# A two-layer encoder kernel: two conditioning blocks moved behind the router, expert rows kept in their order

## The chip, the cores and the metric

The kernel runs on one core of a Trainium2 chip. The metric is the device time of one execution in microseconds (us); lower is better. The core has five engines with instruction streams of their own: PE (TensorE, matrix products), DVE (VectorE), ACT (ScalarE), POOL (GpSimd) and SP (SyncE, which here issues the weight transfers). PEld is PE's weight load. DMA engines move data between device memory and the on-chip memory, and the products are accumulated in a small on-chip memory of their own (PSUM).

## What is computed

Two layers over 256 tokens of width 1024. Each layer has a mixer (linear projections, a bidirectional recurrent branch and an attention branch, merged by gates, an output projection) and a mixture of 32 experts of which each token takes two. Both halves are modulated by a conditioning vector `c`: six vectors per layer, shift, scale and gate, come from `w_ada`. Cut to what matters:

```python
cond = silu(c)
mod = cond @ w_ada[l] + b_ada[l]
shift1, scale1, gate1, shift2, scale2, gate2 = split(mod, 6)
h = rms_norm(x, norm1_g[l]) * (1 + scale1) + shift1
proj = h @ w_in[l] + b_in[l]
...                                   # the two branches, merged
x = x + gate1 * (merged @ w_out[l])
h2 = rms_norm(x, norm2_g[l]) * (1 + scale2) + shift2
p_group = softmax(h2 @ w_router_group[l] + b_router_group[l])   # 4 groups, the best one
e_logits = (h2 @ w_router_expert[l] + b_router_expert[l])       # 8 experts in it, the best two
moe = sum over the two experts of weight * (silu(h2 @ w_gate) * (h2 @ w_up)) @ w_down
x = x + gate2 * moe
```

After the second layer a last `rms_norm` is written out. All weights are float32. `mod` is 12 blocks of 512 columns per layer, two to a vector: blocks 0 to 3 are shift1 and scale1, 4 and 5 gate1, 6 and 7 shift2, 8 and 9 scale2, 10 and 11 gate2. A block's weights are 2 MB, two transfers of 1 MB.

## The kernel before, in words

**Weights.** SP issues the weight transfers in the order of a list, `plan`. Each takes a free place of a ring of 1 MB places (`arena`, 16 of which some hold other data for part of the time; three places `y`, which are `B` in the expert stage; two of `X`) and waits where there is none (`pump`, `fits`, `release`, `withhold`). A place comes free when the last product that reads it is done. When the expert stage begins, nearly all places are open to it.

**Order.** The orders of PE and SP are written out by hand: the instructions of these two stand as the program issues them. Those of DVE, ACT and POOL are placed by a list scheduler by priority (`tc.high_priority` raises it).

**Mixer of a layer** (`mixer`). The activations `xs` (2 x 128 tokens) are turned to columns by 16 products with diagonal matrices `dg` that hold the row scale (`pxt`, L664), and `build` makes from them the input of the projections, each value as a high part `hh` and a low part `hl`. The projections are done in steps (`dense`): a step's weights are cast to a high part by ACT (L495), the rest, the low part, is formed by DVE and POOL (L477), and PE does 24 products of 256 columns (L535). Which step and which piece of the branches follow on each other on PE is a string per layer, `MIX`: a number is so many dense steps, a name is a piece of a branch, and `r6` or `c2` is an ada block of this layer (row) or of the next (column).

**An ada block.** `row(b)` calls `ada_part`: eight products (`pada`, L410) give four partial sums on 128 partitions, ACT copies the sum to a high part (L414), DVE takes the rest (L415). After the next dense step `ada_sum` adds the partitions up by two products with ones (`prow`, L442), and DVE adds the row to `g1b`, `sh2b`, `A2b` or `gt2b` (gate1, shift2, scale2, gate2, each broadcast over the partitions). In layer 1, which has all 12, `MIX` places r4 to r11 in the mixer, and c0 to c3 for the next layer; layer 2 has r6 to r11 there.

**Merge and output projection.** After the last word of `MIX` come eight dense steps of the merge (`pm`, L523) and eight of the output projection (`pd`, L550), in four column pieces n of two steps. Between merge steps 4 and 5 PE turns the row `sh2b` to columns twice, in two orders, by one-row products (`psh` and `psj`, L1064 and L1069); the first serves the router's constant `lc`, the second the rows of the experts. `fin_wo` adds a piece to `xs` and makes `xa` (the row times scale2), `xa_T` turns it (`pxa`), `logits` does the router's products (`pL`, L1089).

**Router and experts** (`experts`). DVE does the row scale for both token halves at once (`rstd_of`), then softmax, the choice of group and experts, and the places of the tokens (`onehot`, L1218), with PE's counting products `pp` (L1180) between. ACT makes the scaled rows `xp[0]` (L1139) from `xa`, reading it in strides to bring it into the order in which the expert weights lie, and DVE the low part `xp[1]` (L1392), both of them in token halves. Then 16 pairs of experts follow, each with `wg`, `wu`, `wd` of 2 MB an expert: gather (`pG`, L1240, once for two pairs), gate and up (`pgu`, L1268), down (`pd`, L1293), scatter (`psc`, L1313). The gather is released by `onehot` and `xp`; the row gate2, `gt2b`, is needed first by the scatter of the first pair.

## Time and profile before

| | us |
|---|---|
| median of 3 runs | 1503.98 |
| lowest and highest | 1502.64, 1508.92 |
| profiled execution, its time | 1508.72 |
| its span in the profile | 1507.0 |
| granted clock of PE over the span | 0.965 |
| PE busy | 1358.7 (90%) |
| DVE busy | 642.6 (43%) |
| ACT busy | 396.0 (26%) |
| POOL busy | 275.9 (18%) |
| weight transfers (SP's queue) | 517.00 MB, 86.4% of the DMA engines' time |

The profile is one execution, and its rows add up to its own span; the time lies 1.7 us above the span. The profiled execution is 4.7 us longer than the median of the three. A share of the whole span says little here, since the program alternates between two kinds of stage: the mixers lie at about 34 to 294 us and 778 to 1020 us, the expert stages behind them. Windows of one stage show which engine is full in it. A row of the trace has the start in us, the duration, the engine, the line, the operation, output <- input and shapes, how many instructions stand in the row (x24), and in brackets how long the engine stood idle ahead of it and what ended that. Neighbours of one kind are drawn together in one row, and a product in full float32 (`pada`, `psh`, `pxt`, `pgu`) counts as two in a trace and as one in the program's order.

### The profile page before, as it was taken

What the parts mean: (1) busy time and instruction counts of PE and PEld (TensorE: products, weight loads), DVE (VectorE), ACT (ScalarE), POOL (GpSimd) and SP (SyncE); (2) the same over time, 40 slices, a digit from 0 to 9 for tenths busy, and PEclk for the clock granted to TensorE, in tenths of its full rate; (3) what the DMA queues carried; (4) which work ended last, traced back from release to release, by engine and by line L of the source; (5) the groups of instructions that cost most, each with busy time, mean ns of one, the idle gap of its engine ahead of it and who ended that gap; (6) DMA issues with size and microseconds to landing.
All of it is one profiled execution on the core that took longest, in us unless ns stands there. A gap on an engine that the chain in (4) does not pass through costs nothing. (4 is left out here: it accounts for less than half of the span.)

```text
span 1507.0 us, 20322 instructions
## 1 busy us (share of the span) xinstructions
PE 1358.7 (90%) x7902; PEld 797.8 (53%) x7903; DVE 642.6 (43%) x1396; ACT 396.0 (26%) x729; POOL 275.9 (18%) x318
## 2 busy tenths in 40 slices
PE   5899999879999989889978999997999999887996
PEld 2877779834434434334347887994434443334432
DVE  1887664632323312223258867554223323213223
ACT  2536554411111101011035366633111111101101
POOL 4644324500000000000015543550000000000000
PEclk9899999989999999989989999998999999999998
DMA  9877687769999999999995657666999999999995
GB/s 330 314 268 245 245 281 281 275 275 422 420 422 421 420 421 422 420 418 375 416 388 193 227 199 256 224 252 227 422 420 421 422 420 422 421 421 419 378 422 218
DMA packets 122633, 522.26 MB, mean 347 GB/s; under 512 B 14068, under 2 KB 16320, under 8 KB 74400
## 3 DMA queue, kind: packets, MB, share of 16 engines
q1 hardware_dynamic: 116448, 517.00, 86.4%
q0 software_dynamic: 1200, 1.99, 0.7%
q10 hardware_dynamic: 4880, 1.87, 0.5%
q8 instruction: 66, 1.08, 0.3%
q14 instruction: 39, 0.32, 0.1%
HBM read 519.77 MB, written 1.05 MB: 346 GB/s over the span
## 5 line engine op out<-in xcount | busy, mean ns | idle before, releaser
L1268 PE MATMUL pgu<-arena 128*64 128x512 f32 x1456 | 349.3, 595 | 20.5 <-DMA arena<-in_w_up_dram 12.0
L1268 PEld LDWEIGHTS pgu<-arena 128*64 128x64 f32 x1456 | 115.4, 137 | 222.8 <-issue 172.8
L1277 DVE SCALAR_TENSOR_TENSOR arena<-pgu,wsl,arena 128x512 f32<-128x512 f32 x32 | 36.4, 1137 | 383.0 <-PE pgu L1268 383.0
L1293 PE MATMUL pd<-arena 128*64 128x512 f32 x720 | 179.8, 597 | 7.3 <-ACT arena L1284 7.3
L1224 POOL TENSOR_TENSOR arena<-oh,arena 128x256 f32<-128x256 f32 x32 | 19.5, 615 | 740.9 <-DVE oh L1218 468.8
L477 POOL TENSOR_TENSOR R<-arena,R 128x512 fp32r<-128x512 f32 (+1 forms) x84 | 124.9, 1490 | 156.3 <-ACT R L495 104.4
L535 PE MATMUL pd<-R,R 128*128 128x256 f32 x1008 | 134.2, 291 | 9.0 <-DVE R L477 5.7
L550 PE MATMUL pd<-R,R 128*128 128x256 f32 x1056 | 136.4, 288 | 2.2 <-DVE R L477 1.9
L535 PEld LDWEIGHTS pd<-R,R 128*128 128x128 f32 x1008 | 127.1, 197 | 18.4 <-issue 6.9
L550 PEld LDWEIGHTS pd<-R,R 128*128 128x128 f32 x1056 | 130.6, 194 | 8.1 <-issue 4.4
L1304 DVE TENSOR_TENSOR y<-pd,arena 128x512 f32<-128x512 f32 x64 | 44.1, 691 | 204.0 <-PE pd L1293 167.7
L1268 PE MATMUL pgu<-B,arena 128*64 128x512 f32 x432 | 118.0, 594 | 2.7 <-DMA B<-in_w_up_dram 2.7
L477 DVE TENSOR_TENSOR R<-arena,R 128x512 fp32r<-128x512 f32 (+1 forms) x100 | 83.3, 840 | 58.5 <-ACT R L495 53.8
L1293 PEld LDWEIGHTS pd<-arena 128*64 128x64 f32 x720 | 56.0, 138 | 95.3 <-issue 85.5
L1305 ACT CAST yh<-y 128x512 fp32r<-128x512 f32 x64 | 39.6, 619 | 241.9 <-DVE y L1304 241.9
L495 ACT CAST R<-arena 128x1024 fp32r<-128x1024 f32 x76 | 79.4, 1046 | 80.5 <-PE pd L550 26.7
L1316 DVE TENSOR_TENSOR xs<-xs,psc 128x512 f32<-128x512 f32 x128 | 79.3, 680 | 17.9 <-PE psc L1313 17.9
L1240 PE MATMUL pG<-oh,X 128*128 128x256 f32 x512 | 74.3, 309 | 13.2 <-DVE oh L1218 9.0
L1240 PEld LDWEIGHTS pG<-oh,X 128*128 128x128 f32 x512 | 70.8, 215 | 24.2 <-issue 24.2
L1268 PEld LDWEIGHTS pgu<-B,arena 128*64 128x64 f32 x432 | 38.4, 137 | 73.2 <-issue 61.2
L1284 ACT COPY arena<-pat 128x512 f32<-128x512 f32 x32 | 18.7, 585 | 220.1 <-PE pat L1283 220.1
L1244 ACT ACTIVATE arena<-pG,sh2c 128x256 f32<-128x256 f32 x64 | 30.3, 474 | 159.0 <-DVE arena L1246 159.0
(328 smaller groups left out, 1694.4 us busy)
## 6 DMA issues: line engine op xcount, KB each, us to landing
arena<-in_w_up_dram SPq DMA_DIRECT2D x104, 1024.0 KB, 19.8
arena<-in_w_down_dram SPq DMA_DIRECT2D x90, 1024.0 KB, 19.8
arena<-in_w_gate_dram SPq DMA_DIRECT2D x78, 1024.0 KB, 19.8
arena<-in_w_ada_dram SPq DMA_DIRECT2D x36, 1024.0 KB, 6.4
B<-in_w_gate_dram SPq DMA_DIRECT2D x30, 1024.0 KB, 19.8
arena<-in_w_in_dram SPq DMA_DIRECT2D x27, 1024.0 KB, 8.2
B<-in_w_up_dram SPq DMA_DIRECT2D x24, 1024.0 KB, 19.8
X<-in_w_gate_dram SPq DMA_DIRECT2D x20, 1024.0 KB, 19.8
```

The lines of the kernel that those rows point to most:

```text
L477: eng.tensor_tensor(dst, full, hi.bitcast(F32), op=ALU.subtract)
L495: A.copy(wh, w)
L535: T.matmul(acc[key][o][:, 0:S], lhsT=w[:, kk, P * o:P * o + P], rhs=x_[:, 4 * kh + kk], start=kh == 0 and i == 0 and kk == 0, stop=kh == 1 ...
L550: T.matmul(acc[key][t][:, 0:256], lhsT=x_[:, 4 * kh + kk, P * t:P * t + P], rhs=w[:, kk], start=kh == 0 and i == 0 and kk == 0, stop=kh == ...
L1240: T.matmul(pG[:, kk, 0:n], lhsT=x_[:, t, k, :], rhs=oh[:, t, :], start=i == 0, stop=i == 3)
L1244: A.activation(xg[k][:, 0:n], pG[:, kk, 0:n], AF.Identity, bias=sh2c[:, k:k + 1])
L1268: T.matmul(pg[CAP * e:CAP * e + CAP, :], lhsT=xg[4 * h + kk][:, P * (i % 2) + CAP * e:P * (i % 2) + CAP * e + CAP], rhs=w[e][:, kk, :], st ...
L1277: V.scalar_tensor_tensor(ac.rearrange("p k q -> p q k"), pu.rearrange("p (q k) -> p q k", k=4), wsl[:, 0:1], sl.rearrange("p (q k) -> p q ...
L1293: T.matmul(pd[n][CAP * e:CAP * e + CAP, :], lhsT=aT[:, 2 * h + kk, CAP * e:CAP * e + CAP], rhs=w[e][:, kk, 512 * n:512 * n + 512], start=h ...
L1304: V.tensor_tensor(y[:, cs], pd, gt2b[:, cs], op=ALU.mult)
L1305: A.copy(yh[:, cs], y[:, cs])
L1316: V.tensor_tensor(xx, xx, pq, op=ALU.add)
```

## The change

1. **gate2 (blocks 10 and 11)** leaves `MIX` in both layers. Its transfers stand in the plan behind the output projection's weights and ahead of the experts'. Its partial sums follow on PE right behind the last logits and stay in two PSUM tiles; ACT copies them to on-chip memory after the router's chain; their sums over the partitions, one product of ones a block in full float32, stand in the first pair, between its gate and its up products.
2. **shift2 (blocks 6 and 7)** stays in `MIX`, but its partial sums go by one strided ACT copy to the order of the experts (`ada_shift`), and after the next dense step eight small products a block turn and sum them at once (`pshift`, `shift_put`). `psh`, `psj` and the row `sh2b` are gone; the constant `lc` is made from a second copy of the router weights, loaded by POOL's queue in the same order (`wr2`).
3. **Rows of the experts**: a third form of `xa`, `xaP`, lies in the experts' order (slot 6 of the arena, which so comes free with slots 4 and 5 behind the low parts). `fin_wo` makes it, by ACT for n = 0 to 2 and by POOL for n = 3. `xp` is then made without strides.
4. **Router chain first**: row scale, logits and `xp` by token half, the chain under a high priority; the low part of the first half ahead of the chain, that of the second behind `onehot`; `weights()` last. The last piece of the output projection is done token half by token half (`by_rows`).
5. **Rows turned unscaled**: `turn_rows` uses plain transposes of `xs`, in layer 1 ahead of the row scale, for layer 2 around the last scatter of layer 1; the scale is spread over the partitions by two products and applied in `build`.
6. **Other**: casts, low parts and ada copies of the mixer get a higher priority (`PREP`); the ring has one more place during the mixer (`spare`, kind `z`, not for expert weights); some parameters of layer 1 go from POOL's queue to SP's; the `MIX` strings have a dense step moved in a few places.

The diff, cut to its core:

```diff
+GATES = (10, 11)
 FIRST = (0, 2, 1, 3)
+PREP = 60
 ORDER = (("q", 2), ("k", 2), ("akv", 1), ("aq", 2), ("v", 2), ("o", 2), ("gm", 4), ("ga", 4))
...
+        if kind == "z":
+            return key[0] not in ("wg", "wu", "wd", "fin")
+        late = key[0] in ("wg", "wu", "wd", "wm", "wa", "wo") or (key[0] == "ada" and key[2] in GATES)
...
+        for b in GATES:
+            plan_ada(l, b)
...
+        return pb
+
+    def ada_part(l, b):
+        pb = ada_sums(l, b)
         ph, pw = parts_at[0][:, 0, :], parts_at[0][:, 1, :]
-        A.copy(ph, pb)
-        V.tensor_tensor(pw, pb, ph.bitcast(F32), op=ALU.subtract)
+        with tc.high_priority(offset=PREP):
+            A.copy(ph, pb)
+            V.tensor_tensor(pw, pb, ph.bitcast(F32), op=ALU.subtract)
         return ph, pw
...
+    def ada_shift(l, b):
+
+        A.copy(turned_sums, ada_sums(l, b).rearrange("p (q k) -> p k q", k=KD))
+
+    def shift_put(sh2c, b3, b):
+        o = 64 * (b % 2)
+        pc = ps.tile([P, 512], F32, tag="f", name="pshift")
+        for k in range(KD):
+            T.matmul(pc[o:o + 64, 2 * k:2 * k + 2], lhsT=turned_sums[:, k, :], rhs=ones[:, 0:2], start=True, stop=True,
+                     tile_position=(0, o))
+        V.tensor_tensor(sh2c[o:o + 64, :], pc[o:o + 64, 0:2 * KD].rearrange("p (k o) -> p k o", o=2)[:, :, 0],
+                        b3[o:o + 64, :], op=ALU.add)
...
+    def turn_rows(pairs):
+        for kp in pairs:
+            pt = turned_rows[kp] = ps.tile([P, 2, S], F32, tag="c", name="pxt")
+            for kk in range(2):
+                for t in range(NT):
+                    k = 2 * kp + kk
+                    T.transpose(pt[:, kk, t * P:t * P + P], xs[:, t, k * P:k * P + P], ident)
...
-            A.copy(wh, w)
-            low(wl[:, 0:2], w[:, 0:2], wh[:, 0:2], V)
-            low(wl[:, 2:4], w[:, 2:4], wh[:, 2:4], G)
+            with tc.high_priority(offset=PREP):
+                A.copy(wh, w)
+                low(wl[:, 0:2], w[:, 0:2], wh[:, 0:2], V)
+                low(wl[:, 2:4], w[:, 2:4], wh[:, 2:4], G)
...
+                    turns_ = [(i, t) for t in range(NT) for i in range(3)]
+                for i, t in turns_:
...
-                    k = 2 * kp + kk
-                    T.matmul(pt[:, kk, t * P:t * P + P], lhsT=xs[:, t, k * P:k * P + P], rhs=dg[t], start=True,
-                             stop=True)
...
+        def spread():
+            pr = ps.tile([P, 512], F32, tag="f", name="pr")
+            for t in range(NT):
+                T.matmul(pr[:, t * P:t * P + P], lhsT=rx[:, t:t + 1].to_broadcast([P, P]), rhs=ident, start=True,
+                         stop=True)
+            V.tensor_copy(scale, pr[:, 0:S])
...
-                src = pts[k // 2][:, k % 2, :]
-                A.activation(hh[:, k, :], src, AF.Identity, bias=c1[:, k:k + 1], scale=A1[:, k:k + 1])
+                src = turned_rows[k // 2][:, k % 2, :]
                 tmp = rot("htmp", 13, 0, 4, S)
-                V.tensor_scalar(tmp, src, A1[:, k:k + 1], c1[:, k:k + 1], op0=ALU.mult, op1=ALU.add)
-                low(hl[:, k, :], tmp, hh[:, k, :], G if k % 2 else V)
+                V.scalar_tensor_tensor(tmp, src, A1[:, k:k + 1], scale, op0=ALU.mult, op1=ALU.mult)
+                A.activation(hh[:, k, :], tmp, AF.Identity, bias=c1[:, k:k + 1])
+                if k % 2:
+                    A.activation(tmp, tmp, AF.Identity, bias=c1[:, k:k + 1])
+                    low(hl[:, k, :], tmp, hh[:, k, :], G)
+                else:
+                    V.scalar_tensor_tensor(hl[:, k, :], tmp, c1[:, k:k + 1], hh[:, k, :].bitcast(F32), op0=ALU.add,
+                                           op1=ALU.subtract)
...
+            cols = p["cols"]
+            V.tensor_tensor(c1, mods[l], cols[:, 80:96], op=ALU.add)
+            with tc.high_priority(offset=100):
+                spread()
+                build(range(8))
...
+            if b // 2 == 3:
+                ada_shift(l, b)
+                last_sum.append(lambda: shift_put(sh2c, p["b3"], b))
+                return
...
+        sh2c = sm.tile([P, KD], F32, tag="sh2c", name="sh2c")
+        nc.gpsimd.dma_start(wr2[:, :, 0:4], w_rg[l].rearrange("(p k) g -> p k g", k=KD))
+        nc.gpsimd.dma_start(wr2[:, :, 4:36], w_re[l].rearrange("(p k) g -> p k g", k=KD))
...
+        xa, xaP = at(5, 0, NT, D), at(6, 0, NT, KD, P)
...
+            dst = xaP[:, t, :, 32 * n:32 * n + 32].rearrange("p k q -> p q k")
+            if n == 3:
+                G.tensor_tensor(dst, xs[:, t, cs].rearrange("p (q k) -> p q k", k=KD),
+                                A2b[:, cs].rearrange("p (q k) -> p q k", k=KD), op=ALU.mult)
+            else:
+                A.copy(dst, xa[:, t, cs].rearrange("p (q k) -> p q k", k=KD))
...
         dense(4)
-        ph = ps.tile([P, 512], F32, tag="c", name="psh")
-        for k in range(KD):
-            T.matmul(ph[:, 2 * k:2 * k + 2], lhsT=sh2b[0:1, P * k:P * k + P], rhs=ones[0:1, 0:2], start=True, stop=True)
...
-        for k in range(KD):
-            T.matmul(pj[:, 2 * k:2 * k + 2], lhsT=sh2b[0:1, :].rearrange("o (q k) -> o k q", k=KD)[:, k, :],
-                     rhs=ones[0:1, 0:2], start=True, stop=True)
...
         assert not any(r[0] is retired[0] for r in ready)
         region("y", f"B{l}", [F32] * 3, "right")
-        release([("y", s) for s in range(3)] + [("a", 6)])
+        release([("y", s) for s in range(3)])
...
-            T.matmul(pL[0][:, 72:108], lhsT=shT[:, k, 0:1].to_broadcast([P, P]), rhs=wr[:, k, :], start=k == 0,
+            T.matmul(pL[0][:, 72:108], lhsT=sh2c[:, k:k + 1].to_broadcast([P, P]), rhs=wr2[:, k, :], start=k == 0,
...
+        gates_ = [ada_sums(l, b) for b in GATES]
...
         ss2 = small("ss2", NT)
-        V.tensor_reduce(ss2, ssn, axis=AX, op=ALU.add)
-        r = rstd_of(ss2, NT, 1.0 / D)
         L = small("L", NT, 36)
         for t in range(NT):
-            V.scalar_tensor_tensor(L[:, t, :], pL[t][:, 0:36], r[:, t:t + 1], lc, op0=ALU.mult, op1=ALU.add)
-        for t in range(NT):
-            A.activation(xp[0][:, t].rearrange("p k q -> p q k"), xa[:, t, :].rearrange("p (q k) -> p q k", k=KD),
-                         AF.Copy, scale=r[:, t:t + 1])
+            V.tensor_reduce(ss2[:, t:t + 1], ssn[:, t, :], axis=AX, op=ALU.add)
+            r = rstd_of(ss2[:, t:t + 1], 1, 1.0 / D, small)
+            V.scalar_tensor_tensor(L[:, t, :], pL[t][:, 0:36], r, lc, op0=ALU.mult, op1=ALU.add)
+            A.activation(xp[0][:, t], xaP[:, t], AF.Copy, scale=r)
+            if t == 0:
+                V.scalar_tensor_tensor(xp[1][:, t], xaP[:, t], r, xp[0][:, t].bitcast(F32), op0=ALU.mult,
+                                       op1=ALU.subtract)
...
+            if not last:
+                turn_rows(range(2))
             scatter(owT, (1,), close)
+            if not last:
+                turn_rows(range(2, 4))
...
-            V.scalar_tensor_tensor(xp[1][:, t].rearrange("p k q -> p q k"),
-                                   xa[:, t, :].rearrange("p (q k) -> p q k", k=KD), r[:, t:t + 1],
-                                   xp[0][:, t].rearrange("p k q -> p q k").bitcast(F32), op0=ALU.mult,
-                                   op1=ALU.subtract)
-        release([("a", 4), ("a", 5)])
+        with tc.issue_after(marks["oh"].ins):
+            marks["lo"] = V.scalar_tensor_tensor(xp[1][:, 1], xaP[:, 1], r, xp[0][:, 1].bitcast(F32), op0=ALU.mult,
+                                                 op1=ALU.subtract)
+        release([("a", 4), ("a", 5), ("a", 6)])
         gather(oh)
-        weights()
+        urgent.close()
+        sums = [at(9, 512 * i, 512) for i in range(2)]
+        for s, pb in zip(sums, gates_):
+            A.copy(s, pb)
+        with tc.issue_after(marks["lo"].ins):
+            weights()
...
+            if i == 0:
+                for h, s in enumerate(sums):
+                    pc = ps.tile([P, 512], F32, tag="f", name="prow")
+                    T.matmul(pc, lhsT=ones, rhs=s, start=True, stop=True)
+                    g = gt2b[:, 512 * h:512 * h + 512]
+                    V.tensor_tensor(g, g, pc, op=ALU.add)
```

**PE in the mixer of layer 1 and in its merge.** Before, the two turns of the shift stand between two merge steps:

```order
L523 MATMUL pm<-Y_1825,R_158 128x256 x2
L523 MATMUL pm<-Y_1826,R_158 128x256
L523 MATMUL pm<-Y_1825,R_158 128x256
L1064 MATMUL psh<-onesr,arena 128x2 x8
L1069 MATMUL psj<-onesr,arena 128x2 x8
L523 MATMUL pm<-Y_1825,R_157 128x256
L523 MATMUL pm<-Y_1826,R_157 128x256
L523 MATMUL pm<-Y_1825,R_157 128x256 x2
```

After, they are gone from there, and behind the dense step that follows on a shift block's `pada` stands `pshift`:

```order
L428 MATMUL pada<-arena,condp 32x512 x8
L596 MATMUL pd<-R_146,R_144 128x256 x8
L596 MATMUL pd<-R_146,R_145 128x256 x8
L596 MATMUL pd<-R_146,R_144 128x256 x8
L455 MATMUL pshift<-onesr,arena 64x2 x8
L878 MATMUL pqt<-ident,arena 128x128 x4
L596 MATMUL pd<-R_147,R_144 128x256 x8
L596 MATMUL pd<-R_147,R_145 128x256 x8
```

The one-row products left the merge, and two groups of eight products of two columns now stand among the dense steps.

**PE behind the last logits.** `pL` are the router's products, `pxa` the last turned rows, `pp` the counting products, which wait for the router's choice. Before:

```order
L1089 MATMUL pL<-arena 128x36 x4
L1052 MATMUL pxa<-ident,arena 128x128 x4
L1089 MATMUL pL<-arena 128x36 x4
L1180 LDWEIGHTS trisb
L1180 MATMUL pp<-arena,trisb 128x64
L1181 LDWEIGHTS onesb
L1181 MATMUL pp<-arena,onesb 128x32
L1183 LDWEIGHTS onesb
L1183 MATMUL pp<-arena,onesb 128x32
```

After:

```order
L1141 MATMUL pL<-arena 128x36 x4
L1115 MATMUL pxa<-ident,arena 128x128 x4
L1141 MATMUL pL<-arena 128x36 x4
L428 MATMUL pada<-arena,condp 32x512 x16
L1238 LDWEIGHTS trisb
L1238 MATMUL pp<-arena,trisb 128x64
L1239 LDWEIGHTS onesb
L1239 MATMUL pp<-arena,onesb 128x32
L1241 LDWEIGHTS onesb
L1241 MATMUL pp<-arena,onesb 128x32
```

The 16 products of the two gate2 blocks now stand where PE waits for the router's choice.

**DVE in the router's chain of layer 1**, from the logits on (`X` are the expert rows, `ry` the row scale). Before, both low parts (L1392) stand in the chain:

```order
L1158 TENSOR_TENSOR arena<-arena,desc 128x64
L1158 TENSOR_TENSOR arena<-arena,desc 128x8
L1392 SCALAR_TENSOR_TENSOR X_2938<-arena,ry,X_2937 128x128x8
L1160 TENSOR_REDUCE arena<-arena 128x8
L1160 TENSOR_REDUCE arena<-arena 128x2
L1392 SCALAR_TENSOR_TENSOR X_2938<-arena,ry,X_2937 128x128x8
L1162 TENSOR_TENSOR arena<-desc,arena 128x64
L1162 TENSOR_TENSOR arena<-desc,arena 128x8
L1200 TENSOR_REDUCE arena<-arena 128x2
L1170 SCALAR_TENSOR_TENSOR arena<-arena 128x64
```

After, the reductions and comparisons stand token half by token half, and one low part (L1197):

```order
L1194 SCALAR_TENSOR_TENSOR arena<-pL,arena,lc 128x36
L1213 TENSOR_REDUCE arena<-arena 128x8
L1197 SCALAR_TENSOR_TENSOR X_2932<-arena,X_2931 128x1024
L1215 TENSOR_TENSOR arena<-arena 128x64
L1213 TENSOR_REDUCE arena<-arena 128x2
L1216 TENSOR_TENSOR arena<-arena,desc 128x64
L1215 TENSOR_TENSOR arena<-arena 128x8
L1218 TENSOR_REDUCE arena<-arena 128x8
L1216 TENSOR_TENSOR arena<-arena,desc 128x8
L1220 TENSOR_TENSOR arena<-desc,arena 128x64
L1218 TENSOR_REDUCE arena<-arena 128x2
L1228 SCALAR_TENSOR_TENSOR arena<-arena 128x64
```

The low part of the second half left this stretch for the place behind `onehot`, and each remaining step has a half of the tokens' width.

## Rows read from the trace of the kernel before

**Rows 1.** Stage windows: layer 1's experts, layer 2's mixer, its router chain, a piece of layer 1.

```profile
318.30:660.00 341.70, 317.60 (x1525) 135.43 (x1523) 98.23 (x167) 40.40 (x72) 7.95 (x13) 0.99 1.01 419
...
786.00:1022.00 236.00, 224.03 (x1766) 203.00 (x1765) 161.35 (x368) 122.74 (x231) 117.13 (x110) 0.97 0.64 229
...
1022.00:1046.30 24.30, 13.25 (x72) 9.57 (x73) 14.87 (x63) 10.32 (x16) 1.19 (x2) 0.72 0.46 173
...
80.00:100.00 20.00, 18.62 (x144) 16.11 (x144) 18.91 (x62) 7.20 (x9) 8.78 (x11) 1.00 0.74 258
```

**Rows 2.** TensorE in the merge of layer 1 (start, duration, what), and the clock window behind it.

```profile
242.75 3.03 PE L523 MATMUL pm<-Y,R 128*128 128x256 f32 x24
...
245.71 1.94 PE L1064 MATMUL psh<-onesr,arena 1*128 1x2 f32 x16
...
247.52 3.94 PE L1069 MATMUL psj<-onesr,arena 1*128 1x2 f32 x16
...
251.38 5.04 PE L523 MATMUL pm<-Y,R 128*128 128x256 f32 x24
...
250.00:252.00 2.00, 2.00 (x10) 1.99 (x10) 0.51 (x2) 0.00 (x0) 0.17 (x1) 0.50 0.00 0
```

**Rows 3.** TensorE, ada blocks 10 and 11 and their row sums.

```profile
178.14 1.06 PE L410 MATMUL pada<-arena,condp 128*32 128x512 f32 x8 [1.38 <-DMA arena<-in_w_ada_dram]
...
849.60 0.78 PE L442 MATMUL prow<-part,onesr 128*128 128x512 f32 x1 [2.25 <-DVE part L415]
...
902.01 1.92 PE L410 MATMUL pada<-arena,condp 128*32 128x512 f32 x16
...
913.03 0.63 PE L442 MATMUL prow<-part,onesr 128*128 128x512 f32 x2
```

**Rows 4.** Around the sum of block 6 in layer 1: VectorE, then TensorE.

```profile
190.67 3.22 DVE L906 SCALAR_TENSOR_TENSOR arena<-arena,ry 128x128 f32<-128x128 f32 x8
...
194.41 0.67 DVE L477 TENSOR_TENSOR R<-arena,R 128x512 fp32r<-128x512 f32 x1
...
194.55 0.79 PE L442 MATMUL prow<-part,onesr 128*128 128x512 f32 x1 [2.88 <-DVE part L415]
...
199.19 2.85 PE L410 MATMUL pada<-arena,condp 128*32 128x512 f32 x16
```

**Rows 5.** The start of the program, TensorE.

```profile
24.01 5.27 PE L664 MATMUL pxt<-arena,xs 128*128 128x128 f32 x32
...
38.95 1.43 PE L535 MATMUL pd<-R,R 128*128 128x256 f32 x5 [2.44 <-ACT R L495]
```

**Rows 6.** TensorE at the border of the two layers.

```profile
770.66 0.40 PE L1313 MATMUL psc<-yl,owT 128*128 128x512 f32 x1
...
777.78 5.47 PE L664 MATMUL pxt<-arena,xs 128*128 128x128 f32 x32 [3.24 <-DVE arena L650]
...
785.49 3.14 PE L535 MATMUL pd<-R,R 128*128 128x256 f32 x24
```

**Rows 7.** Layer 1 from the last output product on: TensorE, SyncE's queue, a DMA window.

```profile
291.24 3.11 PE L550 MATMUL pd<-R,R 128*128 128x256 f32 x24
...
314.77 7.09 PE L1268 MATMUL pgu<-arena 128*64 128x512 f32 x32
...
296.29 22.97 SPq L168 DMA_DIRECT2D arena<-in_w_up_dram  x4
...
318.00:320.00 2.00, 2.00 (x12) 0.60 (x10) 0.00 (x0) 0.00 (x0) 0.00 (x0) 1.00 0.32 66
```

**Rows 8.** Router chain of layer 1: ScalarE, VectorE, TensorE.

```profile
298.30 3.83 ACT L1139 ACTIVATE X<-arena,ry 128x1024 fp32r<-128x1024 f32 x2 [1.12 <-DVE ry L394]
...
300.36 1.97 DVE L1392 SCALAR_TENSOR_TENSOR X<-arena,ry,X 128x1024 fp32r<-128x1024 f32 x1 [0.76 <-ACT X L1139]
...
306.66 0.23 PE L1180 MATMUL pp<-arena,trisb 128*128 128x64 bf16 x1 [8.56 <-DVE arena L1177]
...
308.45 6.39 PE L1240 MATMUL pG<-oh,X 128*128 128x256 f32 x32 [1.47 <-DVE ci L1213]
```

More of the change, by code (lines that the diff above doesn't have):

```diff
@@ L261, in trunk @@
                 plan_ada(l, EARLY[1])
+            if l == 0 and it == ("q", 0, 1):
+                add(("more", l), lambda: first["p"]["more"](), None)
             if it == ("k", 0, 0):
@@ L376, in setup, with rstd_of @@
         return first["p"]
-    def rstd_of(ss, n, scale):
+    def rstd_of(ss, n, scale, place_=None):
         def t(nm):
-            return sm.tile([P, n], F32, tag=f"{nm}{n}", name=nm)
+            return place_(nm, n) if place_ else sm.tile([P, n], F32, tag=f"{nm}{n}", name=nm)
         v, w, y, u = t("rv"), t("rw"), t("ry"), t("ru")
@@ L412, in ada_part @@
             done("ada", l, b, h)
+        return pb
+    def ada_part(l, b):
+        pb = ada_sums(l, b)
         ph, pw = parts_at[0][:, 0, :], parts_at[0][:, 1, :]
-        A.copy(ph, pb)
-        V.tensor_tensor(pw, pb, ph.bitcast(F32), op=ALU.subtract)
+        with tc.high_priority(offset=PREP):
+            A.copy(ph, pb)
+            V.tensor_tensor(pw, pb, ph.bitcast(F32), op=ALU.subtract)
         return ph, pw
     def ada_fast(b):
-        pb = ps.tile([P, 512], F32, tag="f", name="pada")
-        for h in range(2):
-            w = wt("ada", 0, b, h)
-            for kk in range(4):
-                T.matmul(pb[32 * kk:32 * kk + 32, :], lhsT=condp[:, 4 * h + kk, :], rhs=w[:, kk, :],
-                         start=h == 0, stop=h == 1, tile_position=(0, 32 * kk))
-            done("ada", 0, b, h)
         t = rot("fast", 5, 0, 2, 512)
-        A.copy(t, pb)
+        A.copy(t, ada_sums(0, b))
         return t
+    def ada_shift(l, b):
[8 more added lines that the diff above has]
+                        b3[o:o + 64, :], op=ALU.add)
     def ada_put(c1, cols, b, t):
@@ L546, in fn @@
                     acc[key] = [ps.tile([P, 512], F32, tag="f", name="pd") for _ in range(2)]
-                for i, (w, x_) in enumerate(((wh, sh), (wh, sl), (wl, sh))):
-                    for t in range(NT):
-                        for kk in range(4):
-                            T.matmul(acc[key][t][:, 0:256], lhsT=x_[:, 4 * kh + kk, P * t:P * t + P], rhs=w[:, kk],
-                                     start=kh == 0 and i == 0 and kk == 0, stop=kh == 1 and i == 2 and kk == 3)
-                        if kh == 1 and i == 2:
-                            fin(t, acc[key][t][:, 0:256])
+                parts = tuple(enumerate(((wh, sh), (wh, sl), (wl, sh))))
+                turns_ = [(i, t) for i in range(3) for t in range(NT)]
+                if by_rows and kh == 1:
+                    turns_ = [(i, t) for t in range(NT) for i in range(3)]
+                for i, t in turns_:
+                    w, x_ = parts[i][1]
+                    for kk in range(4):
+                        T.matmul(acc[key][t][:, 0:256], lhsT=x_[:, 4 * kh + kk, P * t:P * t + P], rhs=w[:, kk],
+                                 start=kh == 0 and i == 0 and kk == 0, stop=kh == 1 and i == 2 and kk == 3)
+                    if kh == 1 and i == 2:
+                        fin(t, acc[key][t][:, 0:256])
             queue(key, fn)
@@ L694, in mixer @@
         else:
+            cols = p["cols"]
+            V.tensor_tensor(c1, mods[l], cols[:, 80:96], op=ALU.add)
+            with tc.high_priority(offset=100):
+                spread()
+                build(range(8))
             ada_row(l, EARLY[0], pa)
             pa = ada_part(l, EARLY[1])
-            cols = p["cols"]
-            V.tensor_tensor(c1, mods[l], cols[:, 80:96], op=ALU.add)
-            build(range(8))
         if l:
@@ L1100, in mixer, with experts @@
         logits(3)
+        gates_ = [ada_sums(l, b) for b in GATES]
         dump(f"xm{l}", xs)
+        assert not any(r[1][0] == "z" for r in ring.values())
+        free.remove(("z", 0))
         es.close()
         region("x", f"X{l}", [F32] * 2 + [F32R] * 2)
-        return pL, lc, ssn, xa, sh2c
-    def experts(l, p, pL, lc, ssn, xa, sh2c):
+        return pL, lc, ssn, xaP, sh2c, gates_
+    def experts(l, p, pL, lc, ssn, xaP, sh2c, gates_):
         last = l == depth - 1
```

99 lines of the change are left out of this document (48 added, 51 removed).

## Prediction

> **What bounds the kernel now.** I read the stage windows first [rows 1]. In layer 1's expert products the DMA share is 1.01 at 419 GB/s: 341.7 us in which the transfers never stop. PE is busy for 317.6 of them, but its pauses are waits for weights. A place of 1 MB (1.049 million bytes) takes 1.049 / 0.419 = 2.50 us there. An edit that only makes PE, DVE or ACT shorter in that stage is worth nothing, and one that lets the stream start earlier, or keeps it from stopping, is worth what it adds. In layer 2's mixer the picture is turned round: PE 224.0 of 236.0 us, DMA share 0.64, DVE 161.4, ACT 122.7, POOL 117.1. There PE is the bound, its order is written by hand, and each of its waits (12.0 us in that window) is on the path. Between the two lies the router's chain: PE 13.3 of 24.3 us, DVE 14.9, DMA share 0.46. So I price PE time in the mixers at its full length and PE time in the expert stages at nothing, and then ask what the stream makes of an earlier mixer end.
>
> **a. Starts of the layers: -5.0.** In layer 1 the turns (5.27 us) begin at 24.01, and the first dense step waits 2.44 us for a cast until 38.95 [rows 5]. Unscaled turns move into a time in which PE waits, but the chain behind goes through scale, `build` and casts, so not all 5.27 are won; `build` has also four ACT steps more. Between +2 (the steps, where nothing hides them) and -5.3 I take -2.0. At the border the last scatter ends at 771.06, the turns wait 3.24 us for DVE's row scale and begin at 777.78, and dense starts at 785.49 [rows 6]. The turns now stand around the scatter; what is left between is the scale, its spread by two products, and `build`. Of 7.7 us from 777.78 to dense some 3 should go: -3.0, between -1 and -4.5.
>
> **b. The shift's turns in the merge: -10.2.** `psh` takes 1.94 us, `psj` 3.94, and the merge step behind them 5.04 in place of 3.03 [rows 2]. In the window from 250 the granted clock is 0.50, the 1.2 GHz level: PE spent the time before on products of one row and two columns, with which the rows show it as busy all along. Removed per layer: 245.71 to 251.38 is 5.7, and 2.0 for the slow step, 7.7. Added per layer: two groups of `pshift`, each 16 rows of two columns like `psh`, 1.94 each, and no `prow` for the two blocks, 2 x 0.63 [rows 3]. 7.7 - 3.9 + 1.3 = 5.1 a layer.
>
> The Trainium skill (TensorE: Matmul & The Clock Gate, Part 1: The HAM clock gate) says that the low clock is the default and that activity releases it. With that, small products dropped between dense steps could lower the clock anew, at four places instead of two; the last rival prices this from rows.
>
> **c. The gate blocks leave the mixers: -13.8.** A block costs 1.92 us of `pada` and 0.63 of `prow`, four blocks 10.2 [rows 3]. With them go two waits, 1.38 us for a transfer (layer 1) and 2.25 for DVE's part (layer 2). Behind the logits the same products cost nothing: in layer 1 PE stands idle there for 8.56 us until 306.66 [rows 8], and two blocks need 3.84. If that cover went, they would cost 3.8 a layer. Their row sums stand between gate and up products of the first pair, in the stage that the stream bounds: nothing.
>
> **d. Block 6's sum: -3.8.** In layer 1 `prow` waits 2.88 us for DVE, which does 3.22 us of the branches and a low part first [rows 4]; a block a little later takes 2.85 us, against 1.92, so 0.93 is the slow clock behind the wait. A shift block now needs one ACT copy only. If ACT is as late as DVE was, nothing is won; if the neighbouring step is covered too, 5.4.
>
> **e. What DVE gives back: +2.2.** In the piece at 80 to 100 us DVE is busy 18.91 of 20 us, PE 18.62 [rows 1]. There PE runs no faster than DVE. Two of the blocks of c stand in such pieces, and I take back nearly half of their 5.1 us. The other end, where all of the mixers were so, is a rival.
>
> Together 5.0 + 10.2 + 13.8 + 3.8 - 2.2 = 30.6 us less until the two expert stages begin.
>
> **f. What the stream gives back: +7.0.** The stages end when the last weights are in, so what counts is how many weights have landed at T, the end of the last output product: 291.24 + 3.11 = 294.35 in layer 1 [rows 7]. Before, all 18 places are full well ahead of the first free one: a group of four issues that began at 296.29 ends at 319.26, T + 25, and in the window from 318 the DMA share is 0.32. So the stream stands still until the gate products, which begin at 314.77, return places. After, the gate blocks (4 MB) come first and hold four of the 13 places that are open by T. They return them when their sums are done, some 6 us after T; nine expert places are left to fill, 9 x 2.50 = 22.5 us, and the count that stood at T + 25 is reached at T + 28.5. That is 3.5 us a layer. Between 0 (the places return early, or the stream gets ahead in the mixer, which the DMA share of 0.64 would allow) and 10.0 (all four MB of a layer are added to the full stream) I take 3.5, by the count of places.
>
> **g. The router's chain: 0.** The two low parts cost 1.97 us each on DVE, the two strided scalings 3.83 on ACT, and the gather 6.39 at the low clock [rows 8]. Half widths, no strides and one low part behind `onehot` shorten this by perhaps 4 us a layer, and PE, which now has products to do in the wait, may gather at the high clock. But by f the stream is busy until T + 28.5, and the first places come back at about T + 24 even without any gain: the chain has slack. If f were nothing, the 4 us of each layer would count, and the two sizes bound each other.
>
> The added copies (`xaP`), the loads of the router's second weights and the parameters moved to SP's queue lie in mixers with DMA share 0.64 and ACT 122.7 of 236 us [rows 1]: nothing, or a place's 2.50 us where SP's queue is held up once. The higher priority of casts and low parts (`PREP`) can win from the waits that are left or lose in the branches; both are rivals.
>
> **Sum.** 30.6 - 7.0 = 23.6. The profiled execution took 1508.7, so 1485.1 of its kind; it lies 4.7 above the median of 1503.98, so 1480.4, and I say **1481**. The bounds of a, d and f together, which hardly fall on one side at once, give 1476 to 1487 around it.
>
> **Rivals.**
>
> *The mixers are bound by DVE, not by PE (1491).* Then taking products off PE leaves waits for low parts in their place. For it: 18.91 of 20 in the window at 80. Against it: 161.4 of 236 over layer 2's mixer [rows 1]. It would leave a, b and half of c, 5.0 + 10.2 + 6.9 = 22, less 7 for the stream and 2 for shares of b that fall into such pieces: 13 us. Chance 0.20.
>
> *More waits go (1471).* `PREP` puts casts ahead of branch work, and a dense step rarely waits any more. The window of layer 2 has 12.0 us of idle PE; if layer 1 has as much, 24 in all, of which c and d count 6.5. Half of the remaining 17 is 9 to 10 more. Chance 0.13.
>
> *The clock falls at the new small products (1497).* If each of the four `pshift` groups took 3.94 us like `psj` and slowed the next step by 2.0 [rows 2], that would be 4 x 4.0 = 16 us. Against it: `psh` itself took 1.94, and a single group is short. Chance 0.07.
>
> *The gate blocks' transfers are not absorbed (1500).* If all 8 MB are added to the full stream, 8 x 2.50 = 20 us of the 23.6 come back. It needs the stream to be no further at T than before, less the 4 MB, in spite of a shorter wait. Chance 0.06.
>
> *Slower (1514).* `PREP` puts casts and low parts ahead of the branches' chains on ACT and DVE. A low part on DVE is 0.67 us [rows 4] and a cast about 1.0 (half of a strided scaling of 128x1024 [rows 8]), so a chain step that meets one of each is 1.7 late, and with PE's fixed order the dense steps behind it wait. Of the 30.6 - 7.0 = 23.6 us nothing is left at 14 such meetings in both layers, seven a layer; at ten a layer it is 34 - 23.6 = 10 us slower. Against it: casts always stood in the same queues, and the branches' pieces are spread over dense steps. Chance 0.06, with 0.01 for others.
>
> **Chances.** The forecast has 0.48. A measurement of this kernel can tell about 0.5%, 7.5 us, from no change. Faster by more than that: the forecast, the DVE case, the case of more waits, and a little of the clock's, 0.82. Within it: most of the clock's case, the transfers, and tails, 0.11. Slower: 0.07. The range from 1469 to 1497 holds the first four cases.
>
> **What would show it.** Right: no `psh` and `psj`, the merge steps all at about 3.0 us, clock 1.0 in the merge; `pada` right behind the last logits while DVE is at the router; a DMA share near 1.0 from T + 6 on without the dip at 318; dense 2 to 4 us earlier behind the border; mixers shorter by about 15 us each. Wrong: longer idle rows ahead of dense products with DVE or ACT as the releaser; the dip of the DMA share still there, in which case g counts and f does not; `pshift` rows of 4 us; branch products that wait longer than before.

## The result

The median fell from 1504.64 us (4 runs, 1502.64 to 1508.92) to 1484.13 us (4 runs, 1483.02 to 1484.68). The medians differ by 20.5 us. The ratio of the runs is 0.9859, with a 95% interval of 0.9837 to 0.9881, which is 17.9 to 24.5 us less. The forecast was 1481 with a range from 1469 to 1497. The profiled executions differ by more, 1508.72 to 1483.02 (spans 1507.0 and 1481.1, 25.9 us), since the one of before lies 4.1 us above its median and the one of after 1.1 below.

The table sets both profiled executions side by side at five marks on PE: the first dense product, the end of the last output product (T), the first gate product of the experts, the end of the layer's last scatter, and the end of the program. The last column is what the kernel after is ahead by at that mark.

| mark, us | before | after | gained so far |
|---|---|---|---|
| first dense product | 38.95 | 38.20 | 0.8 |
| T in layer 1 | 294.35 | 278.83 | 15.5 |
| first gate product of layer 1 | 314.77 | 295.68 | 19.1 |
| last scatter of layer 1 ends | 771.06 | 757.85 | 13.2 |
| first dense product of layer 2 | 785.49 | 766.26 | 19.2 |
| T in layer 2 | 1021.36 | 994.06 | 27.3 |
| first gate product of layer 2 | 1041.80 | 1009.42 | 32.4 |
| end | 1507.0 | 1481.1 | 25.9 |

The last column is the finding of this case: it rises in the mixers and at the border, rises again in the router's chain, and falls in both expert stages. From T to the last scatter layer 1 takes 479.0 us in place of 476.7, from T to the end layer 2 takes 487.0 in place of 485.6.

### The profile page after: what moved, and what is told of

The parts are those of the page before. It is cut to its first block, busy times and chain, and to the rows that moved or that the text cites. A ratio compares the mean times of both kernels' runs of the same rounds, so it can differ in the third digit from the quotient of the medians.

```text
span 1481.1 us, 20274 instructions
## 1 busy us (share of the span) xinstructions
PE 1345.1 (91%) x7870; PEld 782.3 (53%) x7871; DVE 630.1 (43%) x1390; ACT 399.4 (27%) x749; POOL 281.2 (19%) x321
## 5 line engine op out<-in xcount | busy, mean ns | idle before, releaser
L1328 PE MATMUL pgu<-arena 128*64 128x512 f32 x1520 | 418.6, 594 | 17.7 <-DMA arena<-in_w_up_dram 14.0
L1328 PEld LDWEIGHTS pgu<-arena 128*64 128x64 f32 x1520 | 138.1, 137 | 235.7 <-issue 179.4
L518 POOL TENSOR_TENSOR R<-arena,R 128x512 fp32r<-128x512 f32 (+1 forms) x73 | 108.4, 1486 | 104.0 <-ACT R L537 80.3
L1328 PE MATMUL pgu<-X,arena 128*64 128x512 f32 x240 | 106.6, 594 | 6.4 <-DMA X<-in_w_up_dram 6.4
L518 DVE TENSOR_TENSOR R<-arena,R 128x512 fp32r<-128x512 f32 (+1 forms) x81 | 75.8, 945 | 59.1 <-ACT R L537 49.7
L1328 PE MATMUL pgu<-B,arena 128*64 128x512 f32 x288 | 87.1, 595 | 7.2 <-DMA B<-in_w_gate_dram 5.9
L1300 PE MATMUL pG<-oh,X 128*128 128x256 f32 x512 | 70.6, 298 | 13.0 <-DVE oh L1278 12.0
L537 ACT CAST R<-arena 128x1024 fp32r<-128x1024 f32 x65 | 67.8, 1045 | 51.5 <-PE pd L596 15.5
L1300 PEld LDWEIGHTS pG<-oh,X 128*128 128x128 f32 x512 | 67.0, 204 | 24.1 <-issue 22.6
L1353 PE MATMUL pd<-B,arena 128*64 128x512 f32 x240 | 70.8, 595 | 3.6 <-ACT arena L1344 3.6
```

The lines of the kernel that those rows point to most:

```text
L518: eng.tensor_tensor(dst, full, hi.bitcast(F32), op=ALU.subtract)
L537: A.copy(wh, w)
L1300: T.matmul(pG[:, kk, 0:n], lhsT=x_[:, t, k, :], rhs=oh[:, t, :], start=i == 0, stop=i == 3)
L1328: T.matmul(pg[CAP * e:CAP * e + CAP, :], lhsT=xg[4 * h + kk][:, P * (i % 2) + CAP * e:P * (i % 2) + CAP * e + CAP], rhs=w[e][:, kk, :], st ...
L1353: T.matmul(pd[n][CAP * e:CAP * e + CAP, :], lhsT=aT[:, 2 * h + kk, CAP * e:CAP * e + CAP], rhs=w[e][:, kk, 512 * n:512 * n + 512], start=h ...
```

## The profile after

Windows of the kernel after. Columns as in rows 1: window, length, busy time and instructions of PE, PEld, DVE, ACT, POOL, granted clock, DMA share, GB/s.

```profile
228.00:248.00 20.00, 20.00 (x170) 20.00 (x169) 14.11 (x17) 8.24 (x13) 12.69 (x12) 1.00 0.73 268
278.00:282.00 4.00, 3.14 (x27) 2.82 (x26) 3.85 (x22) 1.66 (x6) 1.95 (x2) 1.00 0.04 16
282.00:286.00 4.00, 3.74 (x34) 0.99 (x33) 3.79 (x20) 2.85 (x4) 0.00 (x0) 1.00 0.44 119
286.00:290.00 4.00, 0.85 (x7) 0.59 (x7) 3.36 (x11) 1.68 (x2) 0.00 (x0) 1.00 1.02 426
298.00:302.00 4.00, 4.00 (x22) 1.31 (x20) 0.46 (x1) 0.00 (x0) 0.00 (x0) 1.00 1.02 426
299.00:640.00 341.00, 312.68 (x1477) 130.51 (x1474) 96.18 (x162) 39.77 (x69) 7.34 (x12) 0.99 1.01 421
766.26:994.06 227.80, 214.00 (x1727) 195.83 (x1723) 161.25 (x364) 126.67 (x243) 116.77 (x113) 0.99 0.65 230
```

The expert stage is as full of transfers as in rows 1 (1.01, 421 GB/s), and the mixer of layer 2 still is PE's: 214.0 of 227.8 us. In the merge (228 to 248) the clock stays at 1.00, where rows 2 show 0.50. What moved is the hole in the stream, the stretch in which no weights come in. Before, it lies from 310 to 318, ahead of the first places that the experts return; a window of it, of the kernel before:

```profile
312.00:314.00 2.00, 2.00 (x12) 2.00 (x12) 0.55 (x2) 0.47 (x1) 0.00 (x0) 0.56 0.00 0
```

Now it lies around T (0.04 and 0.44 from 278 to 286), and from 286 on the stream does not stop. In layer 2 it lies in the same place: from 994 to 1000 the DMA share is 0.03 or less, from 1002 on 0.85 or more.

TensorE of the kernel after in layer 1, from the merge to the first gate products, and one `pshift`:

```profile
123.80 1.09 PE L455 MATMUL pshift<-onesr,arena 128*64 128x2 f32 x16
...
240.27 3.04 PE L565 MATMUL pm<-Y,Y 128*128 128x256 f32 x24
...
275.72 3.11 PE L596 MATMUL pd<-R,R 128*128 128x256 f32 x24
...
282.10 3.64 PE L428 MATMUL pada<-arena,condp 128*32 128x512 f32 x32
287.78 0.20 PE L1238 MATMUL pp<-arena,trisb 128*128 128x64 bf16 x1 [2.04 <-DVE arena L1235]
...
290.52 5.23 PE L1300 MATMUL pG<-oh,X 128*128 128x256 f32 x29 [0.51 <-DVE X L1456]
295.68 3.65 PE L1328 MATMUL pgu<-arena 128*64 128x512 f32 x16
```

T is 275.72 + 3.11 = 278.83. The gate blocks' 3.64 us fit into the wait for the router's choice, of which 2.04 us are left, against 8.56 in rows 8. In layer 2 they take 5.3 us, from 997.33 to 1002.67, in a stretch with the clock at 0.50 in part, and 0.34 us of the wait are left: there they only just fit. The chain from T to the first gate product shrank from 20.4 to 16.9 us, in layer 2 to 15.4.

## The experiments

Four questions stood open. Is the stream what gives time back, and does it hide the router's chain? What is the shift's part worth alone? Where does the border's gain come from, which is twice the forecast? Did the raised priority do anything? Each ratio is taken against runs of the kernel before made beside it; their medians are 1505.49 (the first four), 1505.86 (the part alone, the turned rows, the priority) and 1504.24 (the late turns).

**Gate blocks back in the mixers.** The strings `MIX` are those of before, the blocks' plan position and their sums behind the logits are gone:

```diff
-        for b in GATES:
-            plan_ada(l, b)
...
-        gates_ = [ada_sums(l, b) for b in GATES]
+        gates_ = []
```

> The changed kernel with one part undone: blocks 10 and 11 are summed in the mixers again, where they stood before, and nothing of them stands behind the logits. Theory (the stream and the router's chain share one slack): the two output projections end about 11 to 12 us later in sum, but no gate block holds a place, so the 3.7 us that the stream gave back return, and the chain, shorter by 3.6 and 5.1 us than before, now sets when places come free and counts: 11.6 - 3.7 - 8 is about 0, so within 3 us of the changed kernel's 1484, and the DMA share shows its dip again before the first pair's places come back. Rival (PE time in the mixers counts in full, nothing comes back): 11 to 12 us slower, near 1496.

Measured: 1481.59 us (1479.99 to 1484.67), ratio 0.9839, interval 0.9822 to 0.9855. The largest term of the forecast, taken away, costs nothing; by the medians the kernel is 2.5 us faster without it, but the intervals of the two ratios overlap. In its profile the mixers are 3.0 and 8.2 us longer than in the kernel after, and the expert stages, from T on, 6.2 and 4.4 us shorter. Against the kernel before, the chain is 3.0 and 3.6 us shorter and the expert stages 3.9 and 2.9. Three of its windows, and behind them a row of SP's queue:

```profile
294.00:298.00 4.00, 4.00 (x21) 4.00 (x20) 1.78 (x8) 0.95 (x2) 0.00 (x0) 0.50 0.77 266
298.00:302.00 4.00, 4.00 (x24) 2.10 (x24) 2.02 (x5) 2.23 (x3) 1.19 (x2) 0.98 0.00 0
302.00:306.00 4.00, 4.00 (x20) 1.15 (x16) 0.00 (x0) 0.00 (x0) 0.00 (x0) 1.00 0.51 164
```

```profile
284.22 19.43 SPq L172 DMA_DIRECT2D arena<-in_w_up_dram  x4
```

A group of four issues takes 19.43 us, and the hole is back at 298 to 306, where all places are full and the first gate products have not returned one: here the chain sets the end, and its shortening counts, 6.6 us of chain for 6.8 of the stages. The theory that the stream and the chain share one slack holds, and the rival that counts PE time in full (1496) falls.

**The chain made longer, in both kernels.** Sixteen small steps, each working on the result of the one before:

```diff
+        for _ in range(16):
+            V.tensor_scalar(L, L, 1.0, None, op0=ALU.mult)
         dump(f"L{l}", L)
```

> The changed kernel with 16 small dependent VectorE steps (128x72, about 0.25 us each, 4 us a layer) put into the router's chain. Theory (the chain has slack behind the stream): no change, within 1.5 us of 1484. Rival (the chain counts): 8 us slower, 1492.

> The kernel before with the same 16 steps in its router's chain, 4 us a layer. Theory (there the stream stands still until the first pair's places come back, so the chain counts): about 8 us slower, 1512. Rival (the stream covers the chain there too): no change, 1504.

Measured on the kernel after: 1484.14 us (1483.29 to 1486.11), no change, although its first gate product now comes 20.8 and 21.0 us behind T, 3.9 and 5.7 later than without the steps. Measured on the kernel before: 1515.40 (1510.49 to 1515.72), ratio 1.0068, 1.0051 to 1.0085: 10 us slower. The steps took 0.20 us each, 3.2 us a layer: once they cost nothing, and once more than their own time. Windows of the kernel after with the steps, then of the kernel before with them:

```profile
292.00:296.00 4.00, 1.07 (x7) 0.93 (x7) 3.35 (x10) 0.00 (x0) 0.00 (x0) 0.50 1.01 426
300.00:304.00 4.00, 4.00 (x26) 2.43 (x27) 2.61 (x10) 1.42 (x3) 1.19 (x2) 0.98 1.01 420
304.00:308.00 4.00, 4.00 (x22) 1.29 (x18) 0.00 (x0) 0.00 (x0) 0.00 (x0) 1.00 1.01 422
```

```profile
308.00:312.00 4.00, 4.00 (x21) 4.00 (x21) 0.97 (x2) 0.95 (x2) 0.39 (x1) 0.54 0.00 0
312.00:316.00 4.00, 4.00 (x25) 2.10 (x25) 1.57 (x3) 2.23 (x3) 0.00 (x0) 1.00 0.00 0
316.00:320.00 4.00, 4.00 (x20) 1.15 (x16) 0.00 (x0) 0.00 (x0) 0.00 (x0) 1.00 0.51 158
```

In the first the stream runs through the longer chain at 1.01; in the second it stands still for 8 us at least and waits for the places that the chain's end returns. The chain of that second run grew by 3.1 and 3.3 us in its profile, 6.4 in all, and its expert stages by 1.5 and 3.5. The profiled execution is the shortest of its four; why the median grew by 10 is not explained by it.

**The gate blocks summed earlier.** If the stream sets the end, its start should be worth more than the chain:

```diff
+        gates_ = [ada_sums(l, b) for b in GATES]
         xa_T()
         logits(3)
-        gates_ = [ada_sums(l, b) for b in GATES]
```

> The changed kernel with the sums of blocks 10 and 11 put before the last turned rows and the last logits in place of behind them. It gives four places back some 3 us earlier and makes the router's chain some 3 us longer. Theory (the stream sets the end, the chain has slack): first transfers after the output projection 3 us earlier per layer, 3 to 6 us faster in sum, 1478 to 1481. Rival (the chain is on the path): 6 us slower, 1490.

Measured: 1477.47 us (1476.09 to 1479.89), ratio 0.9817, 0.9800 to 0.9834, 6.7 us under the kernel after. The chain is 2.7 and 3.1 us longer than in the kernel after, and the expert stages are 2.8 and 2.9 us shorter, as the theory says. The windows that answer to those of after:

```profile
282.00:286.00 4.00, 3.10 (x28) 1.61 (x20) 2.39 (x9) 3.97 (x7) 0.00 (x0) 1.00 0.90 336
286.00:290.00 4.00, 0.32 (x4) 0.21 (x4) 3.34 (x20) 0.84 (x1) 0.00 (x0) 0.72 1.01 426
```

The DMA share from 282 to 286 is 0.90 in place of 0.44: of these four us 1.8 more are used for transfers. Against the run with the blocks left in the mixers (1479.99 to 1484.67) no execution overlaps: with the sums here, the move is worth some 4 us.

**The shift's part alone, on the kernel before.** `ada_shift`, `shift_put`, `wr2` and the constant from them; `psh`, `psj` and `sh2b` gone; all else as before:

```diff
+            if b // 2 == 3:
+                ada_shift(l, b)
+                last_sum.append(lambda: shift_put(sh2c, p["b3"], b))
+                return
...
-        ph = ps.tile([P, 512], F32, tag="c", name="psh")
...
-        pj = ps.tile([P, 512], F32, tag="c", name="psj")
```

> The kernel before with one part of the change alone: the shift blocks' sums and turns by small products behind the next dense step, the one-row products gone from the merge. Theory (PE bound mixers, each us counts, and the chain behind is as it was): 5.1 us a layer and the 2.88 us wait with its slow block in layer 1, 14 us in sum, 1490. Rival (VectorE bounds the mixers there): the merge's 7.7 us a layer less the 3.9 of the new products, 7 to 8 us, 1497. Rival (the small products lower the clock): under 3 us, 1501 or more.

Measured: 1489.87 us (1488.19 to 1490.57), ratio 0.9894, 0.9877 to 0.9910: 16.0 us. This part, alone, carries most of what the whole change brings. TensorE around block 6's sum, where rows 4 have the wait of 2.88 us:

```profile
190.41 3.12 PE L556 MATMUL pd<-R,R 128*128 128x256 f32 x24
193.46 1.03 PE L447 MATMUL pshift<-onesr,arena 128*64 128x2 f32 x15
...
196.46 2.11 PE L414 MATMUL pada<-arena,condp 128*32 128x512 f32 x16
```

The wait is gone, and the next block takes 2.11 us in place of 2.85.

**The rows turned by diagonal matrices again, in the kernel after.**

```diff
-    V.scalar_tensor_tensor(tmp, src, A1[:, k:k + 1], scale, op0=ALU.mult, op1=ALU.mult)
-    A.activation(hh[:, k, :], tmp, AF.Identity, bias=c1[:, k:k + 1])
+    A.activation(hh[:, k, :], src, AF.Identity, bias=c1[:, k:k + 1], scale=A1[:, k:k + 1])
```

> The changed kernel with the rows turned by diagonal matrices again, behind the row scale, at both layer starts. If the border's gain of 6.0 us (14.4 to 8.4 us from the last scatter to the first dense product) comes from the unscaled turns, it goes back to 13 to 14.4 us and the kernel is 5 to 7 us slower, 1490; at the program's start under 1 us. If the gain came from priorities or the ring, under 3 us, 1486.

Measured: 1485.57 us (1485.27 to 1486.55), 1.4 above the kernel after, far from 5 to 7. Its marks say why: the border is 14.55 us long again, in place of 8.41, but the first dense product of the program comes at 35.19 in place of 38.20. Two effects of opposite sign had been one term; together they give 3.1 us, of which the medians show 1.4. TensorE of this run at the border, the last scatter and the first dense product:

```profile
754.93 0.40 PE L1369 MATMUL psc<-yl,owT 128*128 128x512 f32 x1
...
769.88 1.34 PE L577 MATMUL pd<-R,R 128*128 128x256 f32 x9
```

TensorE of the kernel after at the start, and behind it a window with the clock:

```profile
24.86 1.93 PE L428 MATMUL pada<-B,condp 128*32 128x512 f32 x8 [1.66 <-DMA B<-in_w_ada_dram]
27.70 1.93 PE L428 MATMUL pada<-B,condp 128*32 128x512 f32 x8 [0.90 <-DMA B<-in_w_ada_dram]
30.31 1.93 PE L428 MATMUL pada<-arena,condp 128*32 128x512 f32 x8 [0.69 <-DMA arena<-in_w_ada_dram]
32.18 3.57 PE L464 MATMUL pcol<-onesr,arena 128*128 128x2 f32 x16
38.20 10.41 PE L577 MATMUL pd<-R,R 128*128 128x256 f32 x72 [2.45 <-ACT R L537]
```

```profile
26.00:30.00 4.00, 2.73 (x12) 0.23 (x8) 0.00 (x0) 0.58 (x1) 0.66 (x1) 0.50 1.05 388
```

The same place with the turns by diagonal matrices, where the clock from 22 to 34 is 1.00:

```profile
29.83 1.04 PE L428 MATMUL pada<-arena,condp 128*32 128x512 f32 x8
30.80 1.95 PE L464 MATMUL pcol<-onesr,arena 128*128 128x2 f32 x16
35.19 4.99 PE L577 MATMUL pd<-R,R 128*128 128x256 f32 x27 [2.44 <-ACT R L537]
```

With its turns done early, PE had nothing left while the last ada blocks landed; it paused three times, the clock fell to 0.50 (1.2 GHz), and the last half block and the turn of its sums took 1.93 and 3.57 us in place of 1.04 and 1.95. That is 2.5 of the 3.0 us. The Trainium skill (TensorE: Matmul & The Clock Gate, Part 1: The HAM clock gate) gives the low clock as the default that activity lifts. The trace agrees here: 0.50 in the window in which PE was busy for 2.73 of 4 us.

**Early sums, and the turns at the start behind the second ada block.** Still unscaled, only later:

```diff
-        if l == 0:
-            turn_rows(range(4))
...
             fast[FIRST[1]] = ada_fast(FIRST[1])
+            turn_rows(range(4))
```

> The run with early sums, and the turns of layer 1's rows moved behind the second ada block at the program's start, still unscaled. Theory (in the changed kernel PE has nothing left to do while the last ada blocks land, its clock is at 0.50 from 26 to 34 us, and the last block's second half and the turn of its sums take 1.93 and 3.57 us in place of 1.04 and 1.95): dense begins at about 35 us in place of 38.0, 3 us faster than with the early sums alone, 1474 to 1475. Rival (ScalarE's four added steps in the build delay the start): dense still at 38, 1477.5.

Measured: 1476.07 us (1474.53 to 1477.78), ratio 0.9814, 0.9798 to 0.9831. TensorE at its start, and a window with the clock:

```profile
30.82 1.95 PE L464 MATMUL pcol<-onesr,arena 128*128 128x2 f32 x16
35.21 5.06 PE L577 MATMUL pd<-R,R 128*128 128x256 f32 x22 [2.45 <-ACT R L537]
```

```profile
26.00:30.00 4.00, 3.43 (x33) 1.28 (x37) 2.77 (x8) 2.42 (x6) 2.44 (x5) 1.00 1.05 385
```

Dense begins at 35.21, so it was the place of the turns and not `build`'s added ScalarE steps, which this run has too. In the profiled execution the mixer behind it is 1.6 us longer than with early sums alone, so of the 3 us only 1.2 are there at T, and the median lies above the 1474 to 1475 expected. Between the two medians, 1.4 us apart, the intervals do not decide. It is the lowest median here, 28 us under the runs of before beside it.

**Without the raised priority.**

```diff
-PREP = 60
+PREP = 0
```

> The changed kernel with the raised priority of casts, low parts and ada copies (PREP) taken away, all else the same. If PREP is what kept the waits ahead of dense products from growing, the mixers become 3 to 8 us longer in sum, 1487 to 1492. If it is worth nothing, 1484. If it put branch work late (the slower rival), the kernel becomes faster, under 1481, and the waits of branch products, 2.85 us ahead of pa in layer 2 the longest, shrink.

Measured: 1483.89 us (1481.08 to 1489.55), ratio 0.9845, 0.9829 to 0.9862: nothing that can be told from the kernel after. Its profiled execution was the longest of its five, so its marks are not used.

## Why the prediction was right

The size of the whole and its main mechanism were right: PE time taken out of the mixers brings T forward, a part of that is given back by the stream, and the chain beside the stream is hidden. Four terms were off by 1 to 3 us each, and their errors nearly cancel; that the sum came so close is in part luck. The signs given for it came, but for the mixers, of which only layer 1's is shorter by some 15 us, and the border, which won more than 2 to 4.

| term, us | forecast | measured in the profiled executions |
|---|---|---|
| start | -2.0 | -0.8 |
| mixer and merge of layer 1 (b to e) | -14.3 | -14.8 |
| border | -3.0 | -6.0 |
| mixer and merge of layer 2 (b, c, e) | -11.3 | -8.1 |
| up to T, in sum | -30.6 | -29.6 |
| given back by the stream (f) | +7.0 | +3.7 |
| whole | -23.6 | -25.9 |

The profile of before has a slow first mixer. In another execution of the same code up to T (the kernel before with the longer chain) it took 251.57 us in place of 255.40; by that one, layer 1's row is -10.9 and not -14.8, against the forecast -14.3, and the whole comes closer to the 20.5 us of the medians.

**a.** The border was sized too small: 14.43 us became 8.41. The other runs agree: 14.4 to 14.6 us in the three with scaled turns, 7.9 to 9.4 in the five with unscaled ones. I let only a share of the time from 777.78 on go and left the 6.7 us ahead of it (a slow ada block, and the wait for the row scale of [rows 6]) as they were. That block in the kernel before:

```profile
770.99 3.55 PE L410 MATMUL pada<-arena,condp 128*32 128x512 f32 x16
```

TensorE of the kernel after there:

```profile
757.45 0.40 PE L1373 MATMUL psc<-yl,owT 128*128 128x512 f32 x1
...
758.76 0.98 PE L504 MATMUL pxt<-ident,xs 128*128 128x128 f32 x7 [0.27 <-DVE xs L1376]
759.67 1.06 PE L428 MATMUL pada<-arena,condp 128*32 128x512 f32 x8
...
766.26 2.18 PE L577 MATMUL pd<-R,R 128*128 128x256 f32 x16
```

The turns are done 1.9 us behind the last scatter and the block behind them runs at the high clock. At the start the sign of the turns themselves was wrong. They cost 3.0 us, most of it by the clock; the 3.8 us from 38.95 to 35.2 (2.9 from the 38.05 of the kernel before with the longer chain) came from what the runs with late turns share with the kernel after, and which of it (the earlier parameters, the added place of the ring) was not tried apart. By those two starts the -0.8 of the table is not clear of noise.

**b.** Confirmed, and a little better. The merge has its steps at 3.04 us and the clock at 1.00, and a `pshift` took 1.09 us, not 1.94 as I took from `psh`; its rows have 64 columns of weights where those of `psh` have 128 [rows 2], but what makes it faster was not tried. The part alone brought 16.0 us; b and d, which it holds, were forecast at 14.0.

**c.** PE's share came: in the mixer of layer 2 its busy time fell by 9.9 us, b and c forecast 10.2 there. The waits did not go with it. Of the 2.25 us ahead of `prow` [rows 3] nothing was won, since others came:

```profile
802.79 1.01 PE L810 MATMUL pa<-ident,al 128*4 128x128 f32 x4 [2.85 <-DVE al L804]
...
843.01 2.30 PE L596 MATMUL pd<-R,R 128*128 128x256 f32 x12 [2.26 <-DVE arena L636]
```

Idle PE in that mixer went from 12.0 to 13.8 us. In other executions of the same mixer it is 14.0 (early sums) and 11.8 (late turns), so it did not fall, and that it rose is not shown. This is in the direction of the rival with VectorE as the bound; the 3 us by which that mixer missed its forecast are no more than the spreads between executions together (235.9 and 237.4 us before, 225.8 to 228.3 after).

**d.** The wait of 2.88 us went; with the part alone too. **e** was not measured by itself.

**f and g.** The mechanism was right: the hole moved to T, the stream then does not stop, the chain's gain is hidden. Adding the 16 steps to the chain costs nothing after and 10 us before. The size of f was twice the measured 3.7. I counted the places as returned 6 us after T, all at once; `pada` begins 3.3 us after T and gives them back half block by half block (its 32 rows take 3.64 us, so the first at about 4.2), and the stream has its share of 0.44 before the last of them. That this is what made f smaller fits the run with early sums, but was not measured by itself. What I had not drawn from my own sentence, that the two sizes bound each other, is that c, f and g are one sum. Without the move of the gate blocks c is lost, but f is lost with it and g counts. The run with the blocks back in the mixers shows the balance at nothing (1481.6 against 1484.1). So the forecast of the whole holds, while the 13.8 us that it credits to the gate blocks are not a gain of that part.

**The rivals.** The clock's case is out: the clock stays at 1.00 in the merge, and the four `pshift` groups take 1.1 to 1.2 us. The transfers of the gate blocks were absorbed but for 3.7 us. My price for that rival was wrong: 7 of its 20 us stood in the sum already, so it would have been 1493 and not 1500. The slower case, casts ahead of the branches, did not occur: the medians with and without the priority are 0.2 us apart. The rows in the experts' order and the router's chain by token halves (points 3 and 4) have no run without them; what the shorter chain is worth is read from the runs above.

## What to carry to other kernels

Where a stage is bound by transfers and the stage before it by an engine, price an edit by the moment at which the stream can run again and by the places that it then finds, and not by the engine's time alone. Work that is moved into a wait holds its buffers until it is done: put it where the buffers come back first, even if the chain beside it grows, as long as the stream covers the chain. Whether a chain has slack is cheap to find out: make it longer by a known time and see whether the end moves.

## What was not expected of the hardware

The same instructions on PE took different times from one execution to the next, and the granted clock differed with them. Windows of the first mixer, of before and of before with the longer chain, which are the same program up to there:

```profile
39.00:255.00 216.00, 203.45 (x1551) 171.68 (x1552) 153.98 (x358) 110.86 (x206) 93.18 (x97) 0.95 0.78 275
```

```profile
38.10:250.00 211.90, 200.30 (x1547) 170.28 (x1548) 153.99 (x358) 111.11 (x206) 93.27 (x97) 0.97 0.80 280
```

PE's busy time is 3.2 us longer at a mean clock of 0.95 than at 0.97, and T came 4.7 us later. That is about the size by which the profiled execution of before lay above its median (4.1 us). So a single profile of a mixer cannot tell differences under some 4 us, and the mixer terms of the table above are no finer than that. What made the clock differ is not shown.
